# Context feed-forward: sums of w2 kept in four PSUM banks over all features, norm tiles lent to weights, decay polynomial issued earlier

## The chip, the cores and the metric

The kernel runs on one core of one Trainium2 chip. The metric is the device time of one execution, in microseconds. Before the change the median of three runs is 2177.3 us (2174.9 to 2180.68).

## The reference

One layer of a diffusion trunk works on 1024 latent tokens and 256 context tokens of width 1024. The stage in question is the first feed-forward, applied to the context:

```
h   = rms_norm(ctx, norm1_w) * (1 + scale) + shift
ctx = ctx + 0.5 * gate * ((silu(h @ w1) * (h @ w3)) @ w2)
```

w1 and w3 have 2816 columns, that is 22 features of 128; w2 has 2816 rows and 1024 columns. After it come the token mixing (retention heads with a decay per head, log_sigmoid of a small table; gated linear attention heads) and a second feed-forward for the latents. The updated context is needed for the mixing; its own second half is not computed.

## The kernel before

All matrices are in fp32. Every operand is split into a high part, which ScalarE writes (L60), and a low part, the rest, which VectorE or GpSimd subtracts (L61). One product is three matmuls (`mm3`, L65 to L67): high by high, high weight by low, low weight by high. Tokens stand on the free axis, so the context is a tile of 256 columns, and the residual stream x of the context is eight tiles of 128 x 256.

The latents' feed-forward runs first. Its w2 part (`back6`) computes six of seven products of a block scheme, in 11 pairs of features each. Behind it comes the context's feed-forward, the stage of the change, and behind that the seventh product (`prod(4)`), the context's keys and values, and the mixing.

In the context's stage a loop runs over f = 0, 2, ..., 20 (`classic`). For each of the features f and f+1 it loads the two halves of w1 (512 columns each) and runs one group of 24 matmuls into a bank of the pool psA (`H`), takes silu on ScalarE (`s1`), does the same with w3, multiplies on VectorE (`s3`, L587) and splits the result into g's high part (`ghi`, ScalarE) and low part (`glo`, VectorE). Between the two features it calls the w2 part of the pair before, `Y(f - 2)`. The last pair's is called in `prod(4)`'s feed.

`Y` (L591 to L614) loads w2 in four halves (two features by two halves of 512 columns). Each of eight units m takes a bank of the pool psB, runs six matmuls (two features, three each), and VectorE adds gate times the sum to x (L600). So a pair has 48 matmuls and eight additions, and the bank is free again when its addition is done.

Weights arrive by SyncE's queue into six `raw` buffers of 256 KB. The high and low parts of w1 and w3 go to the tiles `hh00` to `hh07` and `hl00` to `hl07` (`halves_slots`), which stand free in this stage; those of w2 go to six `whi` and six `wlo` buffers. GpSimd writes the low parts of w1 and w3, VectorE those of w2. Beside all this, VectorE and ScalarE compute the latents' norm (half 1) step by step, one step per pair (`pend`): the sum of squares is summed over partitions by TensorE (L187), `nr` is the power -1/2 of it on GpSimd (L1095), VectorE builds diagonal matrices from it (`ndiag`, L194), TensorE spreads them (L203), and then each of eight features is normed (L217, ScalarE, L223). These products use psB, as `psN` says, and the normed tiles `hh10` to `hl17` are all allocated ahead of the loop.

The order of each engine's instructions is set by a scheduler from the program order, priorities and the times at which it thinks buffers are free; each engine then executes its list in order and waits at the first instruction whose inputs are not there. SyncE's list is written in program order through `back6`.

`lg_setup` (L840 to L871) loads the decay table and computes log_sigmoid with a power on GpSimd and a polynomial in some 25 VectorE operations on tiles of 128 x 8; at L871 and L868 ScalarE takes exponentials of it. It is called by `mix_setup`, at the start of the mixing.

Of the kernel before, what the change touches and what calls it, by code (L numbers as in the profile page):

```python
# [11 lines left out]
F32 = mybir.dt.float32  # L12
F32R = mybir.dt.float32r
AF = mybir.ActivationFunctionType
ALU = mybir.AluOpType
PSUM = bass.MemoryType.PSUM

P = 128
D = 1024
KD = D // P  # L20
DFF = 2816
NF = DFF // P
NP = NF // 2
LAT = 1024
CTX = 256
# [6 lines left out]
class Trunk:  # L32
# [241 lines left out]
    def halves_slots(self, i):  # L274
        if i < 2:
            return None, None
        return tuple(self.hslot(f"0{2 * (i % 4) + j}") for j in range(2))

    def load_halves(self, src, dst=(None, None), eng=None):
        return [self.load_half(src[:, 512 * i:512 * i + 512], dst[i], eng) for i in range(2)]  # L280
# [212 lines left out]
    def back6(self, keep=True):  # L493
        A = self.bank4(self.psA)
        self.prod(1, A, True)
        c1 = self.keep4(A)
        B = self.bank4(self.psB)
        self.prod(2, B, True)
        self.add4(0, 0, self.plus4(c1, B))
        self.prod(6, A, False)  # L500
        u2 = self.keep4(A)
        B = self.bank4(self.psB)
        self.prod(5, B, True)
        c5 = self.keep4(B)
        self.prod(7, A, False)
        if keep:
            u3 = self.keep4(A)
            self.add4(1, 1, self.plus4(c5, u3))
        else:
            self.add4(1, 1, self.plus4(c5, A))  # L510
            self.add4(0, 1, A)
        self.prod(3, B, False)
        self.add4(1, 0, self.plus4(u2, B))
        return A
# [76 lines left out]
    def Y(self, f, order, after=None, qs=(0, 1)):  # L591
# [18 lines left out]
        if after:  # L610
            for tg, o, n in order:
                for m in range(KD):
                    unit(ws[m // 4], tg, o, n, m)
                after(tg, o, n)  # L614

    def H(self, w, tg):
        ps = self.psA()
        self.proj(w, tg, ps)
        return ps
# [217 lines left out]
            act(a, a, AF.Exp, scale=-1.0)  # L837
            act(a, a, AF.Ln, bias=1.0)

    def lg_setup(self):  # L840
        nc, I, cp = self.nc, self.I, self.cp2
        x = self.tile(cp, [P, 8], F32, "lgx")
        nc.sync.dma_start(x, I["decay"].broadcast_to([P, 8]))
        e = self.tile(cp, [P, 8], F32, "lge")
# [5 lines left out]
        t = self.tile(cp, [P, 8], F32, "lgt")  # L850
# [7 lines left out]
            nc.vector.tensor_scalar(out=e, in0=e, scalar1=1.0 / m, scalar2=None, op0=ALU.add)  # L858
        nc.vector.tensor_tensor(out=e, in0=e, in1=u, op=ALU.mult)
        nc.vector.tensor_scalar(out=x, in0=x, scalar1=0.0, scalar2=None, op0=ALU.min)  # L860
        nc.vector.scalar_tensor_tensor(out=x, in0=e, scalar=-2.0, in1=x, op0=ALU.mult, op1=ALU.add)
        self.lg = x
        self.kd = {}
        for i, (nm, s, pos) in enumerate((("f", 0, 2), ("f0", 0, 3), ("b", 4, 0), ("b1", 4, 1))):
            t = self.tile(cp, [P, 4], F32, "kd" + nm)
# [578 lines left out]
    def run(self):  # L1444
        nc, tc, I = self.nc, self.tc, self.I
        S = {}

        def opn(name, side="left"):
            S[name] = tc.tile_pool(name=name, bufs=1, reuse_waits="tile", side=side)
            return S[name].__enter__()  # L1450
# [22 lines left out]
        with tc.manual_schedule(engines={mybir.EngineType.PE, mybir.EngineType.DVE, mybir.EngineType.Activation}):  # L1473
            ws = self.first1((xp, xp, None), n1)
# [24 lines left out]
        hc = opn("hc", "right")  # L1499
        self.gp = hc  # L1500
        n2 = opn("n2", "right")
# [3 lines left out]
        plan = defaultdict(list)  # L1505
# [29 lines left out]
        norm2 = lambda tg, i: norm_step(tg, i, self.mcol(4, int(tg == 2)), self.mcol(3, int(tg == 2)))  # L1535
        for i, at in enumerate((24, 27, 30, *range(33, 33 + KD))):
            plan[at].append(lambda i=i: ctx1(i))

        CT = [(2, 0, 256)]
        p4 = 6 * NP  # L1540
        plan[p4 + 1] += [lambda: self.Y(NF - 2, CT), lambda: self.alloc_h((2,), hc), lambda: norm2(2, 0)]
        plan[p4 + 4].append(lambda: norm2(2, 1))
        plan[p4 + 6].append(lambda: norm2(2, 2))
        for k in range(KD):
# [22 lines left out]
        def spill(tg):  # L1567
            o = TGS[tg][0]
            for k in range(KD):
                nc.sync.dma_start(self.xd[k * P:(k + 1) * P, o:o + 512], self.x[tg][k])  # L1570

        self.alloc_h((1,), self.hp)
        norm2(1, 0)
        pend = [lambda i=i: norm2(1, i) for i in range(1, 3 + KD)] + [lambda: spill(1)]
        for f in range(0, NF, 2):
            self.classic(f, (2,), mid2=(lambda: self.Y(f - 2, CT)) if f else None, eng=[nc.gpsimd if e else None for e in CENG])
            pend.pop(0)()
        A = self.bank4(self.psA)
        self.prod(4, A, True)
        self.add4(0, 1, A)  # L1580
# [85 lines left out]
CENG = (1, 1, 1, 1)  # L1666
# [98 lines left out]
```

## Time and profile before

| what | value |
|---|---|
| median of three runs | 2177.3 us |
| profiled execution, its own time | 2180.54 us |
| its span | 2178.8 us |
| granted TensorE clock, mean | 0.99 |
| first L600 to last | 673.6 to 861.8 us |

The profile has one page and a trace behind it. The page gives busy time per engine, the span in 40 slices, the chain that ended last, and groups of equal instructions with their mean duration and the idle time ahead of them. Answers of the trace give single instructions: start, duration, engine, line, operation, output and inputs, and in brackets how long the engine sat idle before it and what ended that. A matmul's duration in the trace overlaps the next one's; their starts give the pace.

### The profile page before, as it was taken

How to read it: one execution, taken by the hardware profiler on the slowest of the kernel's cores; microseconds unless marked ns; L12 is line 12 of the kernel's file. 1: busy time of each engine (PE TensorE's matmuls, PEld its weight loads, DVE VectorE, ACT ScalarE, POOL GpSimd, SP SyncE). 2: the span in 40 equal slices, each digit the busy share in tenths (PEclk: the TensorE clock that was granted, in tenths of full speed). 3: DMA queues.
4: the chain of work that ended last, by engine and by line, in shares of the span. 5: the costliest groups of instructions: out<-in, count | busy, mean ns of one | idle time of the engine just before them, and what ended most of it. 6: DMA issues, size and time to landing. Idle time of an engine off the chain costs nothing. (4 is left out here: it accounts for less than half of the span.)

```text
span 2178.8 us, 32819 instructions
## 1 busy us (share of the span) xinstructions
PE 2121.3 (97%) x11558; PEld 1811.5 (83%) x11558; DVE 1525.0 (70%) x2735; ACT 980.7 (45%) x1811; POOL 280.4 (13%) x285
## 2 busy tenths in 40 slices
PE   8999999999999999999989999999999999999998
PEld 7888888888889999987778988788878888888888
DVE  7889999756766756834665546758777666675676
ACT  4433334345545444546454335425343433444553
POOL 0000000000026562611132113200000000010000
PEclk8999999999999999999999999999999999999999
DMA  9267768469966565553322312324134444467674
GB/s 331 83 231 239 267 221 268 167 221 325 306 210 193 156 183 171 180 152 100 92 65 63 98 57 88 122 83 162 63 120 161 146 160 159 150 217 251 207 241 147
DMA packets 202933, 373.39 MB, mean 171 GB/s; under 512 B 24016, under 2 KB 37264, under 8 KB 202768
## 3 DMA queue, kind: packets, MB, share of 16 engines
q1 hardware_dynamic: 202336, 371.16, 52.7%
q8 instruction: 90, 1.47, 0.3%
q14 instruction: 75, 0.61, 0.1%
q10 hardware_dynamic: 432, 0.13, 0.0%
HBM read 296.72 MB, written 66.09 MB: 167 GB/s over the span
## 5 line engine op out<-in xcount | busy, mean ns | idle before, releaser
L60 ACT ACTIVATE whi<-raw 128x512 fp32r<-128x512 f32 (+1 forms) x563 | 347.1, 622 | 621.1 <-PE psa L66 169.1
L61 DVE TENSOR_TENSOR wlo<-raw,whi 128x512 fp32r<-128x512 f32 (+1 forms) x533 | 368.1, 694 | 314.3 <-ACT whi L60 310.9
L65 PE MATMUL psa<-hh,whi 128*128 128x512 f32 (+1 forms) x1108 | 435.2, 393 | 0.1
L66 PE MATMUL psa<-hl,whi 128*128 128x512 f32 (+1 forms) x1108 | 434.6, 392 | 0.0
L67 PE MATMUL psa<-hh,wlo 128*128 128x512 f32 (+1 forms) x1108 | 434.3, 392 | 0.0
L65 PE MATMUL psb<-hh,whi 128*128 128x512 f32 (+1 forms) x680 | 260.0, 382 | 0.5 <-ACT whi L60 0.5
L67 PE MATMUL psb<-hh,wlo 128*128 128x512 f32 (+1 forms) x680 | 259.7, 382 | 0.6 <-DVE wlo L61 0.6
L66 PE MATMUL psb<-hl,whi 128*128 128x512 f32 (+1 forms) x680 | 259.7, 382 | 0.0
L65 PEld LDWEIGHTS psa<-hh,whi 128*128 128x128 f32 x1108 | 209.1, 189 | 42.1 <-ACT s L341 0.6
L67 PEld LDWEIGHTS psa<-hh,wlo 128*128 128x128 f32 x1108 | 209.0, 189 | 41.7
L66 PEld LDWEIGHTS psa<-hl,whi 128*128 128x128 f32 x1108 | 209.1, 189 | 41.3
L65 PEld LDWEIGHTS psb<-hh,whi 128*128 128x128 f32 x680 | 127.9, 188 | 25.9 <-ACT whi L60 1.0
L67 PEld LDWEIGHTS psb<-hh,wlo 128*128 128x128 f32 x680 | 127.8, 188 | 25.7 <-DVE wlo L61 1.0
L66 PEld LDWEIGHTS psb<-hl,whi 128*128 128x128 f32 x680 | 127.9, 188 | 24.8
L60 ACT ACTIVATE hh<-raw 128x512 fp32r<-128x512 f32 x180 | 110.4, 623 | 72.7 <-PE psa L66 44.3
L61 POOL TENSOR_TENSOR hl<-raw,hh 128x512 fp32r<-128x512 f32 x84 | 116.2, 1393 | 70.5 <-ACT hh L60 64.4
L1095 POOL TENSOR_TENSOR nr<-nr,mhalf 128x4 f32<-128x4 f32 (+1 forms) x11 | 10.6, 964 | 869.3 <-DVE nr L1094 869.3
L65 PE MATMUL psa<-hh,hh 128*128 128x256 f32 x376 | 107.8, 287 | 0.0
L67 PE MATMUL psa<-hh,hl 128*128 128x256 f32 x376 | 107.8, 287 | 0.0
L66 PE MATMUL psa<-hl,hh 128*128 128x256 f32 x376 | 107.8, 287 | 0.0
L66 PE MATMUL psa<-wlo,hh 128*128 128x256 f32 (+1 forms) x320 | 93.8, 293 | 1.6 <-DVE wlo L61 1.5
L65 PE MATMUL psa<-whi,hh 128*128 128x256 f32 (+1 forms) x320 | 93.5, 292 | 1.2 <-ACT s L1049 1.2
(402 smaller groups left out, 4251.7 us busy)
## 6 DMA issues: line engine op xcount, KB each, us to landing
raw<-in_w SPq DMA_DIRECT2D x374, 256.0 KB, 3.2
gd<-s SPq DMA_DIRECT2D x154, 256.0 KB, 2.8
ada<-in_adaT SPq DMA_DIRECT2D x76, 512.0 KB, 4.8
raw<-gd SPq DMA_DIRECT2D x91, 256.0 KB, 3.0
s<-in_w SPq DMA_DIRECT2D x66, 256.0 KB, 5.0
sd<-s SPq DMA_DIRECT2D x44, 256.0 KB, 2.9
raw<-sd SPq DMA_DIRECT2D x44, 256.0 KB, 3.1
hh<-in_w SPq DMA_DIRECT2D x44, 256.0 KB, 3.9
```

The costliest lines, as they stand in the source:

```text
L60: nc.scalar.activation(hi, src, AF.Copy)
L61: (eng or nc.vector).tensor_tensor(out=lo, in0=src, in1=hi.bitcast(F32), op=ALU.subtract)
L65: mm(ps, wa[0], xa[0], start=start, stop=False, skip_group_check=more)
L66: mm(ps, wa[0], xa[1], start=False, stop=False, skip_group_check=more)
L67: mm(ps, wa[1], xa[0], start=False, stop=stop, skip_group_check=more)
L1095: nc.gpsimd.tensor_tensor(out=r, in0=r, in1=self.mhalf[:, :n], op=ALU.pow)
```

## The change

Four things change. `Yc` takes the place of `Y` for the context: it takes four banks of psB at f = 0 and keeps all eight sums in them (two to a bank), through all 22 features; only in the last pair does VectorE add gate times the sum to x, eight times. The norm's products in the loop go to psA (`psN`). `norm1(k)` allocates the pair of tiles of a normed feature only when it is normed, and until then `halves_slots` lends the tiles `h1{p-2}` to one weight half of pair p, for p from 2 to 9. And the first part of `lg_setup` becomes `lg_start`, called after the loop's step f = 8, with its temporary tiles in the pool `n2`.

```diff
     def halves_slots(self, i):
         if i < 2:
             return None, None
-        return tuple(self.hslot(f"0{2 * (i % 4) + j}") for j in range(2))
+        p, last = i // 4, i % 4 == 3
+        return tuple(self.hslot(f"1{p - 2}" if last and j and 2 <= p < 10 else f"0{2 * (i % 4) + j}") for j in range(2))
...
+    def Yc(self, f):
+        if not f:
+            self.yb = self.bank4(self.psB)
+        ws = {q: [self.load_half(self.w2[f + i][:, 512 * q:512 * q + 512]) for i in range(2)] for q in range(2)}
+        for m in range(KD):
+            ps = self.yb[m // 2][:, m % 2 * CTX:(m % 2 + 1) * CTX]
+            for i in range(2):
+                self.mm3(ps, [t[:, m % 4 * P:(m % 4 + 1) * P] for t in ws[m // 4][i]], self.g[f + i, 2],
+                         not (f or i or m % 2), f == NF - 2 and i == 1, True)
+            if f == NF - 2:
+                x = self.x[2][m]
+                self.nc.vector.scalar_tensor_tensor(out=x, in0=ps, scalar=self.gates_m[1][:, m:m + 1], in1=x,
+                                                    op0=ALU.mult, op1=ALU.add)
...
-    def lg_setup(self):
-        nc, I, cp = self.nc, self.I, self.cp2
+    def lg_start(self, cp):
+        nc, I = self.nc, self.I
...
-        nc.vector.scalar_tensor_tensor(out=x, in0=e, scalar=-2.0, in1=x, op0=ALU.mult, op1=ALU.add)
-        self.lg = x
+        self.lg = self.tile(self.cp, [P, 32], F32, "lg")[:, :8]
+        nc.vector.scalar_tensor_tensor(out=self.lg, in0=e, scalar=-2.0, in1=x, op0=ALU.mult, op1=ALU.add)
+
+    def lg_setup(self):
+        nc, cp, x = self.nc, self.cp2, self.lg
...
-        CT = [(2, 0, 256)]
         p4 = 6 * NP
-        plan[p4 + 1] += [lambda: self.Y(NF - 2, CT), lambda: self.alloc_h((2,), hc), lambda: norm2(2, 0)]
+        plan[p4 + 1] += [lambda: self.Yc(NF - 2), lambda: self.alloc_h((2,), hc), lambda: norm2(2, 0)]
...
-        self.alloc_h((1,), self.hp)
+        self.h[1] = []
         norm2(1, 0)
-        pend = [lambda i=i: norm2(1, i) for i in range(1, 3 + KD)] + [lambda: spill(1)]
+
+        def norm1(k):
+            self.h[1].append(self.hslot(f"1{k}"))
+            norm2(1, 3 + k)
+
+        self.psN = self.psA
+        pend = [lambda i=i: norm2(1, i) for i in (1, 2)] + [lambda k=k: norm1(k) for k in range(KD)] + [lambda: spill(1)]
         for f in range(0, NF, 2):
-            self.classic(f, (2,), mid2=(lambda: self.Y(f - 2, CT)) if f else None, eng=[nc.gpsimd if e else None for e in CENG])
+            self.classic(f, (2,), mid2=(lambda: self.Yc(f - 2)) if f else None, eng=[nc.gpsimd if e else None for e in CENG])
             pend.pop(0)()
+            if f == 8:
+                self.lg_start(n2)
+        self.psN = self.psB
```

The scheduler moves instructions for it (in rows of the changed kernel the line numbers behind the new lines are up to 18 higher, so L1095 reads L1113 there). On TensorE, behind the group of f = 1's w3 (its last two rows come first in both lists; `psa_1373` and `psa_1357` are its bank), there stood before the first group of f = 2:

```order
L66 MATMUL psa_1373_6134<-hl27_823_4102,hh07_1369_6124 128x256
L67 MATMUL psa_1373_6134<-hh27_822_4101,hl07_1370_6125 128x256
L65 MATMUL psa_1384_6184<-hh20_808_4087,hh00_1378_6172 128x256
L66 MATMUL psa_1384_6184<-hl20_809_4088,hh00_1378_6172 128x256
L67 MATMUL psa_1384_6184<-hh20_808_4087,hl00_1379_6173 128x256
```

In the changed kernel Yc(0) stands there, with g of f = 0 (`ghi_1341`, `glo_1342`) and of f = 1 (`ghi_1358`, `glo_1359`; the list is cut at the thirteenth matmul, the first that reads `glo_1359`; the cut ones repeat the pattern for the second and third unit):

```order
L66 MATMUL psa_1357_6118<-hl27_823_4102,hh07_1353_6108 128x256
L67 MATMUL psa_1357_6118<-hh27_822_4101,hl07_1354_6109 128x256
L65 MATMUL psb_1379_6237<-ghi_1341_6063,whi_1384_6243 128x256
L66 MATMUL psb_1379_6237<-glo_1342_6064,whi_1384_6243 128x256
L67 MATMUL psb_1379_6237<-ghi_1341_6063,wlo_1385_6244 128x256
...
L65 MATMUL psb_1379_6237<-ghi_1358_6144,whi_1387_6249 128x256
L65 MATMUL psb_1380_6238<-ghi_1358_6144,whi_1387_6249 128x256
L65 MATMUL psb_1381_6239<-ghi_1358_6144,whi_1393_6261 128x256
L66 MATMUL psb_1379_6237<-glo_1359_6145,whi_1387_6249 128x256
```

So the sums of the first pair move ahead by four groups, 96 matmuls. Those of the second pair move ahead likewise, directly behind the group of f = 3's w3 (`psa_1409`) and three matmuls of the norm; before they stood behind groups of f = 4 and f = 5. The changed kernel's rows (`ghi_1377` is g of f = 2, `ghi_1410` and `glo_1411` that of f = 3):

```order
L67 MATMUL psa_1409_6364<-hh27_822_4101,hl07_1406_6355 128x256
L187 MATMUL psa_1360_6148<-ones_5_84,nacc1_1284_5800 128x1 x3
L65 MATMUL psb_1379_6237<-ghi_1377_6233,whi_1436_6492 128x256
...
L65 MATMUL psb_1381_6239<-ghi_1410_6390,whi_1445_6510 128x256
L66 MATMUL psb_1379_6237<-glo_1411_6391,whi_1439_6498 128x256
```

From Yc(4) on TensorE's order is as before. On GpSimd the norm's `nr` was, before, followed by the last weight split of f = 5 (`hl07_1486`) and preceded by that feature's first three:

```order
L61 TENSOR_TENSOR hl04_1476_6607<-raw_1479_6610,hh04_1475_6606 128x512
L61 TENSOR_TENSOR hl05_1478_6609<-raw_1480_6614,hh05_1477_6608 128x512
L61 TENSOR_TENSOR hl06_1484_6646<-raw_1487_6649,hh06_1483_6645 128x512
L1095 TENSOR_TENSOR nr_1377_6169<-nr_1377_6169,mhalf_6_86 128x4
L61 TENSOR_TENSOR hl07_1486_6648<-raw_1488_6653,hh07_1485_6647 128x512
```

Now all four precede it, and the one that is loaded last, into the lent tile `hl10`, comes first:

```order
L61 TENSOR_TENSOR hl10_1458_6604<-raw_1460_6609,hh10_1457_6603 128x512
L61 TENSOR_TENSOR hl04_1448_6563<-raw_1451_6566,hh04_1447_6562 128x512
L61 TENSOR_TENSOR hl05_1450_6565<-raw_1452_6570,hh05_1449_6564 128x512
L61 TENSOR_TENSOR hl06_1456_6602<-raw_1459_6605,hh06_1455_6601 128x512
L1113 TENSOR_TENSOR nr_1361_6153<-nr_1361_6153,mhalf_6_86 128x4
```

On ScalarE the four halves of w2 of the second pair (`whi_1436`, `whi_1439`, `whi_1442`, `whi_1445`) now stand together, with one weight half of f = 4 (`hh00`) between the last two and the other (`hh01`) behind them. SyncE's loads come in the order of before in this stage.

## The prediction

> **What bounds the kernel now.** I read the page's line of busy times first, to see whether one engine sets the end.
>
> ```profile
> PE 2121.3 (97%) x11558; PEld 1811.5 (83%) x11558; DVE 1525.0 (70%) x2735; ACT 980.7 (45%) x1811; POOL 280.4 (13%) x285
> ```
>
> TensorE is busy for 97% of the span of 2178.8 us. The change leaves the number of its weight products alone, so only two things can bring the end nearer: shorter gaps on TensorE, and less time at half clock. I therefore cut the context's feed-forward (until about 860 us) into stretches. The columns are start and end, length, then busy us and instructions of PE, PEld, DVE, ACT and POOL, then the granted clock, DMA share and GB/s.
>
> ```profile
> 660.00:680.00 20.00, 17.40 (x143) 16.99 (x142) 11.01 (x19) 10.62 (x22) 16.06 (x11) 1.00 0.65 199
> 680.00:700.00 20.00, 20.00 (x145) 20.00 (x144) 10.71 (x20) 8.62 (x16) 11.25 (x9) 0.83 0.57 177
> 700.00:720.00 20.00, 16.32 (x119) 16.12 (x118) 18.11 (x28) 9.17 (x17) 7.55 (x5) 0.85 0.41 119
> 720.00:740.00 20.00, 18.90 (x152) 18.49 (x152) 18.91 (x26) 10.62 (x20) 12.28 (x8) 0.98 0.51 154
> 740.00:760.00 20.00, 20.00 (x170) 20.00 (x168) 9.63 (x18) 9.24 (x18) 11.89 (x9) 1.00 0.61 189
> ```
>
> From 740 us on TensorE issues 170 matmuls in 20 us, 0.1176 us each. The four stretches ahead of that hold 143 + 145 + 119 + 152 = 559, where that pace would give 680. The 121 missing ones are **14.2 us**, all that this stage has to give. Then I asked the view by line who waits for the gated addition to x (L600): its row, and the engine that waited for it (us, times); and the timeline of TensorE for the four waits themselves (the bracket is idle time and releaser).
>
> ```profile
> L600 DVE SCALAR_TENSOR_TENSOR x<-psb,modc,x x88: 466/472/486, 673.6 to 861.8; 128x256 f32<-128x256 f32 x88
> ...
>   PE psb L65: 7.3, 4
> ```
>
> ```profile
> 674.15 0.39 PE L65 MATMUL psb<-ghi,whi 128*128 128x256 f32 x1 [0.72 <-DVE x L600]
> 679.17 0.39 PE L65 MATMUL psb<-ghi,whi 128*128 128x256 f32 x1 [1.88 <-DVE x L600]
> 715.15 0.58 PE L65 MATMUL psb<-ghi,whi 128*128 128x256 f32 x1 [3.67 <-DVE x L600]
> 736.15 0.39 PE L65 MATMUL psb<-ghi,whi 128*128 128x256 f32 x1 [0.99 <-DVE x L600]
> ```
>
> All 7.3 us fall into the first three pairs of features, where the latents' norm keeps VectorE full (18.1 and 18.9 of 20 us above) and L600 stands in its queue. The remaining 7 us are mostly half clock behind the waits, which finer stretches show:
>
> ```profile
> 675.00:680.00 5.00, 3.12 (x26) 2.91 (x25) 2.52 (x4) 3.14 (x6) 4.21 (x3) 0.99 0.58 182
> 680.00:685.00 5.00, 5.00 (x26) 5.00 (x25) 3.66 (x9) 1.39 (x3) 2.28 (x2) 0.50 0.55 178
> 715.00:720.00 5.00, 4.85 (x22) 4.85 (x23) 4.21 (x10) 0.72 (x1) 0.00 (x0) 0.50 0.13 46
> 720.00:725.00 5.00, 5.00 (x40) 5.00 (x40) 4.18 (x7) 2.57 (x5) 1.76 (x2) 0.92 0.32 105
> ```
>
> At full pace 5 us hold 42.5 matmuls. Behind the wait of 3.67 us the slow clock cost (42.5 - 22 + 42.5 - 40) x 0.1176 = 2.7 us, 2.6 without the wait's last 0.15.
>
> **What the change removes.** 80 of the 88 L600 go, and with them every wait for a bank that one of them holds: the sums lie in four banks until the last pair. That takes the waits and the slow clock behind them, **-14.2 us**. The 80 x 0.472 = 38 us of VectorE work saved count for no more than that, since TensorE waits for VectorE nowhere else in this stage. The last eight additions follow their sums one by one, as before: 0.
>
> **What it puts in: the first sums stand too early.** The instruction order puts Yc(0) directly behind f=1's second group, where four more groups (96 matmuls) used to be. In the trace that place is at 660.21; Yc(0)'s thirteenth matmul, twelve further on, would stand at 661.65, and it needs the low half of g of f=1.
>
> ```profile
> 660.21 0.28 PE L65 MATMUL psa<-hh,hh 128*128 128x256 f32 x1
> ...
> 661.65 0.28 PE L65 MATMUL psa<-hh,hh 128*128 128x256 f32 x1
> ```
>
> ```profile
> 662.42 0.42 ACT L60 ACTIVATE ghi<-s 128x256 fp32r<-128x256 f32 x1 [1.59 <-DVE s L587]
> 662.87 0.63 DVE L61 TENSOR_TENSOR glo<-s,ghi 128x256 fp32r<-128x256 f32 x1 [0.48 <-ACT ghi L60]
> 664.57 0.40 ACT L60 ACTIVATE ghi<-s 128x256 fp32r<-128x256 f32 x1
> 665.01 1.26 DVE L61 TENSOR_TENSOR glo<-s,ghi 128x256 fp32r<-128x256 f32 x1 [0.92 <-ACT ghi L60]
> ```
>
> VectorE's order up to these rows is the same in both kernels, so nothing brings them sooner: g's low half is there at 665.01 + 1.26 = 666.27, and TensorE is 4.6 us late. It waits in pieces (for 662.84, 663.50, 664.97 and 666.27), so half clock may add up to 2.6.
>
> **The second sums stand too early as well, and behind a longer chain.** Yc(2) follows f=3's second group directly. Its thirteenth matmul stands 158 behind Yc(0)'s start, so without any delay at 660.21 + 158 x 0.1176 = 678.8. It needs g of f=3, whose low half stands on VectorE behind the first `ndiag`, which waits for GpSimd's `nr`, and there four weight splits (f=5's) now stand ahead of `nr`, the first of them for the load that comes last. These are the rows for that chain; the two group rows have count, busy us and mean ns, and the DMA row size and median us to landing.
>
> ```profile
> 669.16 0.63 ACT L60 ACTIVATE whi<-raw 128x512 fp32r<-128x512 f32 x1 [3.66 <-DMA raw<-in_w]
> 669.88 0.69 DVE L61 TENSOR_TENSOR wlo<-raw,whi 128x512 fp32r<-128x512 f32 x1 [3.61 <-ACT whi L60]
> 671.29 0.97 DVE L61 TENSOR_TENSOR wlo<-raw,whi 128x512 fp32r<-128x512 f32 x1 [0.72 <-ACT whi L60]
> ```
>
> ```profile
> L61 POOL TENSOR_TENSOR hl<-raw,hh 128x512 fp32r<-128x512 f32 x84 | 116.2, 1393 | 70.5 <-ACT hh L60 64.4
> ...
> raw<-in_w SPq DMA_DIRECT2D x374, 256.0 KB, 3.2
> ```
>
> ```profile
> 682.02 0.16 DVE L1094 TENSOR_SCALAR nr<-psb 128x4 f32<-128x4 f32 x1 [0.44 <-PE psb L187]
> 682.26 1.01 POOL L1095 TENSOR_TENSOR nr<-nr,mhalf 128x4 f32<-128x4 f32 x1 [2.40 <-DVE nr L1094]
> 683.42 1.56 DVE L194 TENSOR_SCALAR ndiag<-ident,nr 128x128 f32<-128x128 f32 x2
> ```
>
> The four halves of w2 now stand together in ScalarE's order. The second one's low part ends at 671.29 + 0.97 = 672.26 and frees the buffer for the fourth; 3.2 for that load and 0.63 for its split give 676.1. Behind it ScalarE splits f=4's second half (0.63, 676.7), GpSimd takes 1.39 for its low part (678.1), and this frees the buffer of f=5's last load: 3.2 and 0.63 more, 681.9. Then four GpSimd splits (5.6, 687.5), `nr` (1.0), `ndiag` (0.8) and the low half of g (0.6): 689.9. So TensorE is **11.1 us** late there. This contains the 4.6 of Yc(0) and its half clock, which only shorten the second wait. Bounds: if the splits do not stand in the way, `nr` follows f=3's sum of squares at 660.21 + 4.6 + 145 x 0.1176 = 681.9, with 0.16 + 1.0 + 0.8 + 0.6 behind, hence 684.5 and 5.7 us; if each split takes the 2.26 of the slowest row (660.96, below), 3.5 more, 14.6. I take 11.1: it uses the mean row.
>
> ```profile
> 660.96 2.26 POOL L61 TENSOR_TENSOR hl<-raw,hh 128x512 fp32r<-128x512 f32 x1 [5.68 <-ACT hh L60]
> ```
>
> **Half clock behind Yc(2).** TensorE's wait there is 11.1 - 4.6 = 6.5 us, or 3.9 if Yc(0) already cost 2.6. The trace knows both outcomes: 3.67 us was followed by half clock (above), a lone 2.44 us at 1124.68 was not, as the stretch behind it shows.
>
> ```profile
> 1124.68 0.30 PE L1081 MATMUL psb<-ident,t 128*128 128x128 f32 x1 [2.44 <-DVE t L1327]
> ...
> 1126.00:1131.00 5.00, 5.00 (x34) 4.49 (x33) 4.59 (x9) 1.28 (x4) 0.00 (x0) 1.00 0.32 96
> ```
>
> Both waits are nearer to the first, so I take **2.6** (ends 0 and 2.6). The Trainium skill, "TensorE: Matmul & The Clock Gate" (section "Why this matters for your kernels"), warns of idle gaps over about 3 us alone. By that rule Yc(0)'s pieces, 2.4 us at most, cost no clock and Yc(2)'s 6.5 us do, so it speaks against this change at the same place. The trace agrees on the 3.67 and the 2.44; on the slow clock behind 0.72 and 1.88 us (680 us above) it goes beyond the rule.
>
> **The smaller edits.** One `ndiag` stands behind f=5's product on VectorE (0.41 + 0.78 at most, TensorE has a few matmuls in between): 0.5, ends 0 and 1.2. From Yc(4) on TensorE's order is the old one: 0. The decay's polynomial moves from the start of the mixing to the end of the first latents' stage.
>
> ```profile
> 937.41 0.40 PE L66 MATMUL psa<-wlo,hh 128*128 128x288 f32 x1 [1.18 <-DVE wlo L61]
> 941.03 0.21 ACT L871 ACTIVATE cdec<-lgx 128x8 f32<-128x8 f32 x1 [7.63 <-DVE lgx L861]
> 455.00:475.00 20.00, 20.00 (x89) 16.44 (x88) 12.84 (x20) 6.08 (x12) 0.00 (x0) 1.00 0.58 192
> ```
>
> There the weight split that TensorE awaits stands between its small operations: **-1.2** (0 if another wait takes the place). At its new place (about 458 to 472 us) VectorE has 7.2 of 20 us free and TensorE waits for nothing, so 0; if that cover were gone, up to 1.5, the wait for GpSimd's power in the chain. The small load passes SyncE's queue there once its buffer is free: in the same 0 to 1.5. The new slots for weight halves add no instruction; what they do to the order is in the chain above.
>
> **Sum:** -14.2 + 11.1 + 2.6 + 0.5 - 1.2 = **-1.2 us**. The profiled run was 2180.5 (span 2178.8), which gives 2179.3; against the median of 2177.3, **2176.1**.
>
> **Rivals.**
> - The short chain: f=5's loads come early enough, or its splits do not delay `nr`, and Yc(2) costs only the lower bound. -14.2 + 5.7 + 0.5 - 1.2 = -9.2, 2168.1; with half clock behind Yc(0), 2170.7. For it: GpSimd was busy for only 11.3 of 20 us at 680. Against: the rows of the chain.
> - The long chain without half clock behind it: -3.8, 2173.5.
> - Slower: the four w2 halves in a row make ScalarE wait in every pair. The third and fourth wait for a buffer that VectorE frees (0.69), a load (3.2) and a split (0.63): 4.5 us, in which the next pair's silu stands behind them, and the last group of that pair waits for the bank that this silu reads. One group (24 x 0.1176 = 2.8) lies between, so at most 1.7 us a pair, 15 in the nine pairs from Yc(4) on: 2191. It ends over 0.3% slower from 0.86 a pair. Against: ScalarE has over 10 of 20 us free at 740.
> - The change does not do what it says: L600 was only the last of several waits, and weights or g end as late. 2177. Against: the waits name L600 four times, and from 740 on, with the same loads, TensorE never waits.
>
> **How the numbers follow.** 0.3% (6.5 us) is about what a measurement of this kernel tells from no change. Forecast 0.37, short chain 0.30, long chain at full clock 0.15, slower 0.13, no effect 0.05. The short chain alone is faster by over 0.3%: 0.30; forecast, full clock and no effect lie within: 0.57; slower 0.13. The range runs from 2165 (the short chain with the decay's polynomial gaining more) to 2184: it takes in the chain's upper bound (+3.5, 2179.6) with 1.5 at the polynomial's new place and the clock's uncertain terms, and leaves out the 0.13 and a little of the short chain.
>
> **What would show it.** Right: no wait of TensorE for a gated addition before the last pair; idle time at about 660 to 666 and again at 683 to 690, the second released by g of f=3, with clock 0.50 behind it; 170 matmuls per 20 us from there on; no wait at the start of the mixing for the low half of a weight. Wrong: Yc(2) starting without a wait, or waits for silu in the later pairs.

## The result and the profile after

The changed kernel takes 2189.98 us (median of six runs, 2187.8 to 2195.8), the kernel before 2179.86 in the same comparison (six runs, 2174.9 to 2182.32). The ratio is 1.0053 with an interval of 1.0036 to 1.0069: **slower by 10 to 12 us** (10.1 by the medians, 11.6 by the ratio), where 2176.1 (2165 to 2184) was predicted. TensorE's busy time grew with the span (2188.4 us):

```profile
PE 2126.1 (97%) x11558; PEld 1808.4 (83%) x11558; DVE 1510.5 (69%) x2655; ACT 976.9 (45%) x1811; POOL 280.5 (13%) x285
```

The same stretches as in the prediction, and the four behind them, of the changed kernel (length; busy us and instructions of PE, PEld, DVE, ACT, POOL; granted clock; DMA share; GB/s):

```profile
660.00:680.00 20.00, 16.34 (x110) 15.54 (x110) 9.71 (x16) 9.29 (x18) 9.80 (x7) 0.83 0.62 193
680.00:700.00 20.00, 17.85 (x151) 17.65 (x150) 5.88 (x12) 8.24 (x16) 10.66 (x10) 1.00 0.52 161
...
740.00:760.00 20.00, 20.00 (x171) 20.00 (x170) 11.08 (x10) 8.50 (x18) 11.40 (x8) 1.00 0.53 170
760.00:780.00 20.00, 18.47 (x156) 18.26 (x155) 11.03 (x10) 9.53 (x20) 12.12 (x9) 1.00 0.51 159
780.00:800.00 20.00, 18.40 (x156) 18.19 (x154) 11.46 (x11) 9.73 (x21) 12.62 (x10) 1.00 0.52 159
800.00:820.00 20.00, 18.61 (x157) 18.41 (x156) 12.84 (x12) 9.26 (x19) 13.73 (x11) 1.00 0.57 175
820.00:840.00 20.00, 18.52 (x154) 18.11 (x152) 7.96 (x10) 8.71 (x17) 11.51 (x9) 1.00 0.60 187
```

Up to 680 us the cost stands where the prediction put it, and 740 to 760 is full. But the four stretches from 760 on lose some 1.5 us each, where the kernel before lost nothing (its row for the same 80 us):

```profile
760.00:840.00 80.00, 80.00 (x669) 80.00 (x668) 39.72 (x75) 39.13 (x75) 47.40 (x36) 1.00 0.61 182
```

The changed kernel's waits of TensorE in this stage, from its timeline:

```profile
664.52 0.58 PE L65 MATMUL psb<-ghi,whi 128*128 128x256 f32 x1 [3.56 <-ACT ghi L60]
...
689.75 0.39 PE L66 MATMUL psb<-glo,whi 128*128 128x256 f32 x1 [2.15 <-DVE glo L61]
...
766.24 0.39 PE L66 MATMUL psb<-glo,whi 128*128 128x256 f32 x1 [1.53 <-DVE glo L61]
...
785.19 0.38 PE L66 MATMUL psb<-glo,whi 128*128 128x256 f32 x1 [1.60 <-DVE glo L61]
...
803.92 0.39 PE L66 MATMUL psb<-glo,whi 128*128 128x256 f32 x1 [1.39 <-DVE glo L61]
...
821.54 0.39 PE L66 MATMUL psb<-glo,whi 128*128 128x256 f32 x1 [0.27 <-DVE glo L61]
...
841.07 0.38 PE L65 MATMUL psb<-ghi,whi 128*128 128x256 f32 x1 [2.28 <-ACT ghi L60]
```

No matmul waits for a gated addition any more. The first two waits are Yc(0)'s and Yc(2)'s; a norm product's wait of 0.45 us for `ndiag` at 707.14 is left out. The later ones lie 18 to 20 us apart, one in each pair of features, 7.1 us together; the sum had nothing for them.

To see where the 10 us arise, I set the two traces beside each other matmul by matmul (by line, operands and order) and subtracted the starts. The difference of the starts, changed minus before, grows in these stretches (times of the kernel before):

| stretch of the kernel before, us | growth, us | what lies there |
|---|---|---|
| 0 to 640 | +0.6 | latents' feed-forward |
| 640 to 748 | -4.5 | Yc(0), Yc(2), the L600 waits gone |
| 748 to 853 | **+9.1** | the waits in the pairs |
| 853 to 928 | +0.1 | seventh product |
| 928 to 958 | -1.3 | old place of the decay's polynomial |
| 958 to 1600 | +0.7 | mixing |
| 1600 to 1940 | **+4.5** | second feed-forward of the latents |
| 1940 to 2150 | +0.5 | end |

So there are two losses, and the second lies in a stage that the change does not touch. There TensorE waits for nothing in either kernel; its rows for 240 us of that stage, before and then changed:

```profile
1700.00:1940.00 240.00, 240.00 (x1061) 198.72 (x1060) 162.27 (x265) 97.99 (x170) 0.00 (x0) 1.00 0.47 155
```

```profile
1700.00:1940.00 240.00, 240.00 (x1047) 196.11 (x1046) 159.17 (x261) 94.41 (x164) 0.00 (x0) 1.00 0.45 148
```

Busy throughout at full clock, and still 14 matmuls fewer: 0.2267 us from start to start before, 0.2297 now. The groups say which. First the kernel before, then the changed one, in that window (count, busy us and mean ns):

```profile
L65 PE MATMUL psa<-hh,whi 128*128 128x512 f32 x104 | 40.5, 389 | 0.0
...
L67 PE MATMUL psa<-t3h,wlo 128*128 128x512 f32 x25 | 9.7, 389 | 0.0
```

```profile
L65 PE MATMUL psa<-hh,whi 128*128 128x512 f32 x104 | 40.5, 389 | 0.0
...
L67 PE MATMUL psa<-t3h,wlo 128*128 128x512 f32 x28 | 11.1, 395 | 0.0
```

Matmuls whose moving operand lies in `t1` to `t3` became slower, those with `hh` did not. Of the two groups of tiles, `hh` and the weights lie in pools that grow from the left, and `t1` to `t3` in one from the right. The change put the permanent tile `lg`, 128 bytes in each partition, ahead of the left ones: `hh00` moved from byte 3200 to 3328 and the first `whi` from 81024 to 81152, while `t1h0` stayed at 163712. The distance from weight to `t` went from a multiple of 256 bytes to 128 off one.

For the pairs I read ScalarE's timeline ahead of the wait at 766.24, then VectorE's, in the changed kernel:

```profile
759.76 1.67 ACT L60 ACTIVATE hh<-raw 128x512 fp32r<-128x512 f32 x3 [5.68 <-DMA raw<-in_w]
761.34 0.37 ACT L582 ACTIVATE s<-psa 128x256 f32<-128x256 f32 x1
```

```profile
761.74 0.42 DVE L588 TENSOR_TENSOR s<-psa,s 128x256 f32<-128x256 f32 x1 [5.76 <-ACT s L582]
762.93 1.85 DVE L223 SCALAR_TENSOR_TENSOR hl<-nt,modl,hh 128x512 fp32r<-128x512 f32 x1 [0.78 <-ACT hh L218]
764.71 1.48 DVE L61 TENSOR_TENSOR glo<-s,ghi 128x256 fp32r<-128x256 f32 x1
```

ScalarE sits idle for 5.68 us at a weight split that waits for its load. Two more splits and silu (L582) stand behind it, then VectorE's product, a norm step, and g's low half, which ends at 764.71 + 1.48 = 766.19; TensorE goes on at 766.24. The order shows which load it is. ScalarE's rows there in the changed kernel (`hh14` is the lent tile; `hh04`, `hh05` and `hh06` belong to the same feature):

```
L60 ACTIVATE hh14_1658_7597<-raw_1661_7603 128x512
L60 ACTIVATE hh04_1648_7556<-raw_1652_7560 128x512
L60 ACTIVATE hh05_1650_7558<-raw_1653_7564 128x512
L582 ACTIVATE s_1606_7353<-psa_1605_7328 128x256
L60 ACTIVATE hh06_1656_7595<-raw_1660_7599 128x512
```

The last number of a load gives its place in SyncE's order: the split that stands first needs the load that comes last (7603 behind 7560, 7564 and 7599). It can stand first because its tile is free early; a tile of the ring `hh00` to `hh07` comes free only when the pair before has used it.

The same order stands in all eight pairs with a lent tile, from f = 4 on. From the second of them on, ScalarE's wait at the lent half grows, and TensorE waits only from the 5.68 us above on (behind it they are 4.69, 4.55, 3.45 and 4.57). The three ahead of it:

```profile
702.52 1.68 ACT L60 ACTIVATE hh<-raw 128x512 fp32r<-128x512 f32 x3 [1.33 <-DMA raw<-in_w]
...
722.08 1.67 ACT L60 ACTIVATE hh<-raw 128x512 fp32r<-128x512 f32 x3 [2.42 <-DMA raw<-in_w]
...
739.79 1.67 ACT L60 ACTIVATE hh<-raw 128x512 fp32r<-128x512 f32 x3 [3.59 <-DMA raw<-in_w]
```

**Theory**: two separate causes. The lent tile's split stands ahead of its load's turn (about 9 us), and 128 bytes moved two operands of one matmul against each other (about 5 us). **Rivals**: the pair waits come from w2's four halves standing together (the prediction's slower case); the slower pace comes from something else that the change does, such as the early decay or the four banks; or Yc(0) and Yc(2) alone make the loss.

### The profile page after: what moved, and what is told of

Same layout as the page of the kernel before. It is cut to its first block, busy times and chain, and to the rows that moved or that the text cites. A ratio compares the mean times of both kernels' runs of the same rounds, so it can differ in the third digit from the quotient of the medians.

```text
span 2188.4 us, 32748 instructions
## 1 busy us (share of the span) xinstructions
PE 2126.1 (97%) x11558; PEld 1808.4 (83%) x11558; DVE 1510.5 (69%) x2655; ACT 976.9 (45%) x1811; POOL 280.5 (13%) x285
## 5 line engine op out<-in xcount | busy, mean ns | idle before, releaser
L61 DVE TENSOR_TENSOR wlo<-raw,whi 128x512 fp32r<-128x512 f32 (+1 forms) x533 | 375.9, 710 | 332.6 <-ACT whi L60 327.7
L65 PE MATMUL psa<-hh,whi 128*128 128x512 f32 (+1 forms) x1108 | 435.3, 393 | 0.0
L67 PE MATMUL psa<-hh,wlo 128*128 128x512 f32 (+1 forms) x1108 | 434.7, 392 | 0.0
L65 PE MATMUL psb<-hh,whi 128*128 128x512 f32 (+1 forms) x680 | 260.0, 382 | 0.5 <-ACT whi L60 0.5
L67 PE MATMUL psb<-hh,wlo 128*128 128x512 f32 (+1 forms) x680 | 259.9, 382 | 0.4 <-DVE wlo L61 0.4
L65 PEld LDWEIGHTS psa<-hh,whi 128*128 128x128 f32 x1108 | 209.2, 189 | 42.5 <-ACT s L342 0.4
L67 PEld LDWEIGHTS psa<-hh,wlo 128*128 128x128 f32 x1108 | 209.2, 189 | 41.9
L65 PEld LDWEIGHTS psb<-hh,whi 128*128 128x128 f32 x680 | 127.8, 188 | 26.3 <-ACT whi L60 1.0
L67 PEld LDWEIGHTS psb<-hh,wlo 128*128 128x128 f32 x680 | 127.7, 188 | 25.7 <-DVE wlo L61 0.8
L65 PE MATMUL psa<-hh,hh 128*128 128x256 f32 x376 | 106.2, 282 | 0.0
L67 PE MATMUL psa<-hh,hl 128*128 128x256 f32 x376 | 105.9, 282 | 0.0
L65 PE MATMUL psa<-whi,hh 128*128 128x256 f32 (+1 forms) x320 | 93.2, 291 | 3.3 <-ACT s L1067 3.0
L67 PE MATMUL psa<-whi,hl 128*128 128x256 f32 (+1 forms) x320 | 92.4, 289 | 0.0
```

The lines of the kernel that those rows point to most:

```text
L61: (eng or nc.vector).tensor_tensor(out=lo, in0=src, in1=hi.bitcast(F32), op=ALU.subtract)
L65: mm(ps, wa[0], xa[0], start=start, stop=False, skip_group_check=more)
L67: mm(ps, wa[1], xa[0], start=False, stop=stop, skip_group_check=more)
```

## The experiments

Twelve kernels ran, in three groups on one chip each, each group with its own runs of the kernel before. Before gave medians of 2177.18, 2179.32 and 2175.61 in the three, and single runs of one kernel lie up to 6.5 us from their median, so I compare ratios, above all between groups. The last three columns are growths from the aligned traces as in the table above, each against the one profiled execution of the kernel before.

| kernel | median, us | ratio to before (95%) | 640-748 | 748-853 | 1600-1940 |
|---|---|---|---|---|---|
| changed | 2189.98 | 1.0053 (1.0036 to 1.0069) | -4.5 | +9.1 | +4.5 |
| e1_addr | 2184.40 | 1.0036 (1.0022 to 1.0049) | -2.8 | +9.3 | 0.0 |
| e2_shift | 2186.49 | 1.0045 (1.0032 to 1.0058) | +1.5 | -1.1 | +4.5 |
| e3_nolend | 2176.47 | 0.9998 (0.9989 to 1.0007) | -6.7 | -1.2 | +4.5 |
| e4_lend | 2183.46 | 1.0026 (1.0015 to 1.0037) | -6.7 | +6.3 | 0.0 |
| e5_both | 2170.56 | 0.9967 (0.9956 to 0.9979) | -6.3 | 0.0 | 0.0 |
| e6_late | 2172.71 | 0.9973 (0.9964 to 0.9983) | -6.1 | 0.0 | 0.0 |
| e7_lendfirst | 2176.94 | 0.9992 (0.9983 to 1.0001) | -7.6 | 0.0 | +4.5 |
| e8_shift256 | 2182.68 (one run) | | -0.3 | 0.0 | 0.0 |
| e9_align | 2168.56 | 0.9966 (0.9953 to 0.9978) | -7.2 | 0.0 | 0.0 |
| e10_order | 2164.56 | 0.9949 (0.9935 to 0.9962) | -13.5 | 0.0 | 0.0 |
| e11_best | 2164.31 | 0.9948 (0.9935 to 0.9961) | -12.3 | 0.0 | 0.0 |
| e12_lg | 2182.28 | 1.0022 (1.0011 to 1.0033) | -2.2 | 0.0 | 0.0 |

The three growth columns are not equally sure. That one execution of the kernel before took 2180.54 us, some 3 us over its median. In 640 to 748 the kernels with TensorE's order of before and no lent tile (e2_shift, e8_shift256, e12_lg) scatter from -2.2 to +1.5, as the waits and the half clock behind them fall, so a difference of under some 4 us in that column shows nothing by itself. In the other two columns the kernels without a loss agree within about 0.1, but for the -1.1 and -1.2 that are explained below.

### The 128 bytes: e1_addr, e2_shift, e8_shift256

e1_addr is the changed kernel with `lg` in a pad at the right-hand edge, so that every other tile lies where it lay before; the order of all engines is that of the changed kernel.

```diff
-        self.lg = self.tile(self.cp, [P, 32], F32, "lg")[:, :8]
...
-        self.pad(edge, 24)
+        self.pad(edge, 16)
+        self.lg = self.tile(edge, [P, 8], F32, "lg")
```

> The changed kernel with the eight columns of `lg` kept in a corner of the right-hand pad instead of a tile of 128 bytes in the permanent pool. All weight, hidden and norm tiles of the feed-forwards stand at the addresses of before again; every engine's order is that of the changed kernel. Address theory (the 128-byte shift slows the 128x512 matmuls of the latents' feed-forwards): start to start 0.2267 us again in the second feed-forward (0.2297 after), about 5 us faster than the changed kernel, 2185 where that is 2190. Rival (the slower pace comes with the run, or from the loads): 2190, pace 0.2297.

e2_shift is the kernel before with an unused tile of 128 bytes in the same pool; e8_shift256 has one of 256 bytes (`[P, 64]`).

```diff
+        nc.gpsimd.memset(self.tile(cp, [P, 32], F32, "shift"), 0.0)
```

> The kernel before with an unused tile of 128 bytes per partition at the end of the permanent pool, so that the same tiles stand 128 bytes higher, as after; one memset on GpSimd at the start is added and every engine's order is else that of before. Address theory: 5 us slower than before, pace 0.2297 in the second feed-forward. Rival: as before, pace 0.2267.

> The kernel before with an unused tile of 256 bytes instead of the 128 of e2_shift; all orders as in e2_shift. If any shift of the weights against the unshifted tiles t1 to t3 slows those matmuls: 0.2297 us start to start at 1700 to 1940 us, 0.233 with t1 to t3. If only some distances do (weights and t lie 256 bytes apart modulo 512 before, 128 in the changed kernel, 0 here): 0.2267.

The same 240 us in e1_addr, e2_shift and e8_shift256:

```profile
1700.00:1940.00 240.00, 240.00 (x1060) 198.82 (x1059) 161.08 (x264) 97.64 (x170) 0.00 (x0) 1.00 0.47 152
```

```profile
1700.00:1940.00 240.00, 240.00 (x1047) 196.12 (x1046) 158.65 (x260) 94.89 (x165) 0.00 (x0) 1.00 0.44 147
```

```profile
1700.00:1940.00 240.00, 240.00 (x1060) 198.80 (x1059) 161.15 (x264) 97.64 (x170) 0.00 (x0) 1.00 0.46 152
```

1060, 1047, 1060, against 1061 before and 1047 after. An unused tile of 128 bytes alone brings the slow pace into the kernel before, one of 256 bytes does not, and the change at its old addresses has the old pace. So the pace of this stage hangs on the distance of the operands, and not on the change's work. By the ratios the shift is worth 0.0017 in the changed kernel (1.0053 against 1.0036, 3.7 us) and 0.0031 without the lending (e3_nolend against e5_both below, 6.7 us); the traces have 4.5. The 9.3 us (2186.49 - 2177.18) that e2_shift lost are more than its 4.5 here and 1.3 ahead of 640 us; its trace has 3.1 more in the mixing. But e8_shift256, at the old pace, has 1.9 there, and e5_both 2.6, so that part is no effect of the pace. In e2_shift and e5_both 1.6 of it is half clock behind one wait, the 2.44 us at 1124.68 of the kernel before, which came in seven of the fourteen traces and not in the others; the rest stays open.

Nor does a shift by 128 bytes always cost. In the pairs the 128x256 matmuls of e2_shift and e3_nolend start every 118.7 ns, where the kernel before has 120.0; that is their -1.1 and -1.2 in 748 to 853. e7_lendfirst, with the same shift, has 118.7 only until about 700 us and then 120.0, so distance alone doesn't settle the pace there.

### The lent tile: e3_nolend, e7_lendfirst, e4_lend

e3_nolend is the changed kernel without the lending. e7_lendfirst lends the same tiles to the half that is loaded first of the four instead of last.

```diff
-        p, last = i // 4, i % 4 == 3
-        return tuple(self.hslot(f"1{p - 2}" if last and j and 2 <= p < 10 else f"0{2 * (i % 4) + j}") for j in range(2))
+        return tuple(self.hslot(f"0{2 * (i % 4) + j}") for j in range(2))
```

> The changed kernel without the lending: weight halves go to the tiles 00 to 07 only, as before; Yc, the norm on psA and the early decay stay. TensorE's, GpSimd's and SyncE's orders are those of the changed kernel, ScalarE's and VectorE's differ in some twenty rows. Lending theory (ScalarE's splits for a lent tile stand ahead of silu and wait there for their load): the five waits of 1.4 to 2.3 us for g in the pairs after 760 us and the half clock at 840 go, 7 to 9 us faster than the changed kernel. Rival (Yc itself, or its w2 halves in a row, make g late in each pair): the waits stay, within 1 us of the changed kernel. The first two waits (665 and 689 us) stay in both.

```diff
-        p, last = i // 4, i % 4 == 3
-        return tuple(self.hslot(f"1{p - 2}" if last and j and 2 <= p < 10 else f"0{2 * (i % 4) + j}") for j in range(2))
+        p, lend = i // 4, i % 4 == 2
+        return tuple(self.hslot(f"1{p - 2}" if lend and not j and 2 <= p < 10 else f"0{2 * (i % 4) + j}") for j in range(2))
```

> The changed kernel with the lent tile given to the first-loaded half of f + 1 in each of the pairs 2 to 9 (w1's, instead of w3's second, which is loaded last of the four). Addresses as after. Order theory (the harm comes from the last-loaded half standing first in ScalarE's order, silu behind it): the waits for g after 760 us go although a tile is lent, and the time is within 2 us of e3_nolend, 2176.5. Rival (the lending itself harms, by the norm's steps or by buffers held): the waits stay, 2184 to 2190.

e4_lend is the kernel before with the lending and the late allocation of the norm's tiles alone.

> The kernel before with the lending alone: weight halves of pairs 2 to 9 in tiles 10 to 17 until these are normed; Y and its additions as before. Only ScalarE's and VectorE's orders differ from before, by some twenty rows. Lending theory: waits of TensorE for g appear in the pairs after 760 us, 5 to 9 us slower than before. Rival (the waits need Yc): no wait for g, 0 to 1 us from before.

The stretch of the pairs in e3_nolend, e7_lendfirst and e4_lend:

```profile
760.00:840.00 80.00, 80.00 (x677) 80.00 (x676) 30.26 (x44) 39.22 (x75) 42.63 (x32) 1.00 0.61 186
```

```profile
760.00:840.00 80.00, 80.00 (x669) 80.00 (x669) 33.96 (x47) 40.40 (x78) 43.19 (x32) 1.00 0.58 177
```

```profile
760.00:840.00 80.00, 77.63 (x630) 75.83 (x629) 49.18 (x81) 37.88 (x74) 45.33 (x32) 1.00 0.55 172
```

Without the lending, or with it for the first-loaded half, TensorE never idles here; with it alone, in the kernel before, it does. By the ratios e3_nolend is 0.0055 (12 us) faster than the changed kernel, more than the 7 to 9 us expected, and e7_lendfirst lies within 0.0006 of e3_nolend: the lending costs by its place in the order, not by its presence. In the traces 10.3 us of the difference to e3_nolend lie in the pairs and 2.2 at 640 to 748, where the wait at 689.75 is. This also rules out the first rival: in e3_nolend ScalarE still waits for w2's loads (27.7 us in 15 waits over 650 to 845 us), and TensorE does not wait for ScalarE in the pairs. e4_lend lost 6.3 us by time, and 6.3 in the pairs by its trace. The expectation had waits for g there; in fact there is one, of 1.12 us at 835.83, and the others are for gated additions, which are still there in this kernel (1.05 us at 747.58, 0.51 at 765.99, the rest about 0.1). So it shows that the lending costs without Yc, but in part through other waits; that e4_lend's profiled execution was still no longer (span 2177.9) comes from 640 to 748 us, where that one execution lost less to half clock (granted 0.98 over 660 to 760, before 0.93), and one profile can't tell whether the next would.

The lending also made the wait at 689.75: in e3_nolend TensorE's waits for g add up to this in the whole stage, 0.20 of it at Yc(2), where the changed kernel has 2.15 at Yc(2) alone:

```profile
PE psb L65 <- ACT ghi L60: 3.6, 1, 3.6
PE psb L66 <- DVE glo L61: 0.5, 2, 0.2
```

It made it on VectorE. The rows for `nr`, `ndiag` and g's low half, in the changed kernel and then in e3_nolend:

```profile
688.02 1.01 POOL L1113 TENSOR_TENSOR nr<-nr,mhalf 128x4 f32<-128x4 f32 x1
...
689.07 0.29 DVE L194 TENSOR_SCALAR ndiag<-ident,nr 128x128 f32<-128x128 f32 x1 [2.81 <-POOL nr L1113]
689.27 0.42 DVE L61 TENSOR_TENSOR glo<-s,ghi 128x256 fp32r<-128x256 f32 x1
```

```profile
687.78 1.22 DVE L61 TENSOR_TENSOR glo<-s,ghi 128x256 fp32r<-128x256 f32 x1 [0.25 <-ACT ghi L60]
...
688.68 1.19 POOL L1112 TENSOR_TENSOR nr<-nr,mhalf 128x4 f32<-128x4 f32 x1
...
689.90 0.48 DVE L194 TENSOR_SCALAR ndiag<-ident,nr 128x128 f32<-128x128 f32 x2 [0.90 <-POOL nr L1112]
```

GpSimd's `nr` comes no sooner without the lending, since the four splits stand ahead of it there too. But in the changed kernel the first `ndiag` stands ahead of g's low half, which so waits for `nr`; in e3_nolend it stands behind.

### Both undone, and the early sums: e5_both, e6_late, e10_order

e5_both joins the edits of e1_addr and e3_nolend.

> e1_addr and e3_nolend together: the changed kernel without the lending and with the tiles at the addresses of before. If the two causes add: 5 to 6 us below e3_nolend (2176.5), so 2171, and the decay's early start still gains 1.3 at 940 us. If the slower pace of e3_nolend's second feed-forward hid something else: 2174 to 2177.

It is **faster than the kernel before** (0.9967), so four banks over all features do pay, with the early decay that it still has (its stretch at 928 to 958 gains 1.6 us). What is left in its stage is Yc(0)'s wait (3.4 us) and half clock behind it. e6_late is e5_both with Yc(0) and Yc(2) at a low priority, so that the scheduler puts their matmuls where their inputs are ready.

```diff
+    def Yl(self, f):
+        with self.low(100 if f < 4 else None):
+            self.Yc(f)
```

> e5_both with Yc(0) and Yc(2) at a lower priority in the scheduler, so that Yc(0) stands behind the groups of f = 3, where Y(0) stood before, and Yc(2) behind f = 5 and 6. Early-sums theory (their place costs 4.6 us of waiting and 2.3 at half clock at 665 us): no wait at 661 to 669 us, no half clock there, 6 us below e5_both. Rival (the sums only wait elsewhere, for w2's buffers or for nr): 0 to 2 us below, with new waits of TensorE before 740 us.

Its waits of TensorE from 650 to 865 us (us in total, times, longest):

```profile
PE psa L187 <- DVE nacc L178: 2.9, 1, 2.9
PE psa L203 <- DVE ndiag L194: 2.5, 2, 2.3
PE psa L65 <- ACT s L581: 0.2, 1, 0.2
```

The waits moved on to the norm's products (L187, L203), which now came too early in their turn: 5.6 us in place of 3.6, and no gain. e10_order therefore moves all of it: TensorE keeps program order in the loop, the norm's steps come one pair later, and the store of x (`spill`) comes behind the loop.

```diff
-        pend = [lambda i=i: norm2(1, i) for i in (1, 2)] + [lambda k=k: norm1(k) for k in range(KD)] + [lambda: spill(1)]
-        for f in range(0, NF, 2):
-            self.classic(f, (2,), mid2=(lambda: self.Yc(f - 2)) if f else None, eng=[nc.gpsimd if e else None for e in CENG])
-            pend.pop(0)()
-            if f == 8:
-                self.lg_start(n2)
+        pend = [lambda: None] + [lambda i=i: norm2(1, i) for i in (1, 2)] + [lambda k=k: norm1(k) for k in range(KD)]
+        with self.pe_order():
+            for f in range(0, NF, 2):
+                self.classic(f, (2,), mid2=(lambda: self.Yc(f - 2)) if f else None, eng=[nc.gpsimd if e else None for e in CENG])
+                pend.pop(0)()
+                if f == 8:
+                    self.lg_start(n2)
+            spill(1)
```

> e5_both with TensorE's order in the context's loop written out in program order, and the norm's steps one pair later: Yc(0) stands behind f = 2's two groups, the sum of squares behind f = 3's. Early-place theory, with what e6_late taught (the norm's product must move too): no wait at 661 to 669 us and no half clock, 5 us below e5_both's 2170.6. Rival (each move uncovers the next wait): a wait of about the same size elsewhere before 740 us, 0 to 2 us.

All of TensorE's waits in its stage (650 to 865 us), and the first 100 us of it:

```profile
PE psa L203 <- DVE ndiag L194: 0.3, 1, 0.3
```

```profile
660.00:760.00 100.00, 99.67 (x832) 99.47 (x831) 57.92 (x75) 55.15 (x107) 69.43 (x49) 1.00 0.62 192
```

TensorE is full at clock 1.00, and the stage gains 13.5 us against the kernel before. By time it is 11.1 us faster than before (2164.56 against 2175.61).

### Another distance, the best version, and the decay alone: e9_align, e11_best, e12_lg

In the first feed-forward the tiles of x lie 224 bytes off a multiple of 256 from the weights (96 off in the changed kernel). e9_align is e5_both with an empty tile of 224 bytes ahead of them.

```diff
+        self.tile(self.dp, [P, 56], F32, "gap")
```

> e5_both with 224 bytes more in the right-hand pool of the first feed-forward, so that there the sixteen x tiles stand a multiple of 256 bytes from the weight tiles (96 modulo 256 instead of 128 before, against weights at 128). All orders unchanged. Distance theory (a matmul is slower where its two operands' distance is no multiple of 256 bytes): matmuls with x as operand at 200 to 400 us go from about 0.234 to 0.227 us, some 2 us below e5_both. Rival (x is slow there for another reason, as its loads): no difference.

(The expectation has the two residues the wrong way round: x stood at 96 modulo 256 and now stands at 128, as the weights do.) The x matmuls in 120 to 440 us, before and then in e9_align:

```profile
L65 PE MATMUL psa<-x,whi 128*128 128x512 f32 x50 | 20.2, 404 | 0.0
...
L67 PE MATMUL psa<-x,wlo 128*128 128x512 f32 x50 | 19.8, 396 | 0.0
```

```profile
L65 PE MATMUL psa<-x,whi 128*128 128x512 f32 x54 | 21.5, 398 | 0.0
...
L67 PE MATMUL psa<-x,wlo 128*128 128x512 f32 x53 | 20.6, 389 | 0.0
```

They became faster and its trace is 3.3 us ahead of before by 640 us, where e5_both was 0.5 behind. But the ratio (0.9966) is e5_both's (0.9967): by time the gain isn't shown. e11_best joins e9_align and e10_order:

> e9_align and e10_order together. If both theories hold: 7 us below e5_both, 2163 to 2164. If only one: 2166 to 2169.

At 0.9948 (0.9935 to 0.9961) it beats both kernels, and can't be told from e10_order. e12_lg is the kernel before with the early decay alone (`lg_start` behind f = 8, `lg` in the right-hand pad).

> The kernel before with the early decay alone, its result in a corner of the right-hand pad, so that nothing is shifted. Expected from the prediction's term: the wait of 1.18 us for the low half of a weight at 937 us goes, 1.2 to 1.6 us below before. Rival (the chain delays VectorE where it now stands): as before or slower, with a wait of TensorE at 455 to 480 us.

It was slower, 1.0022. The rival had that, but for another reason: at the polynomial's new place its trace gained no wait. The old wait at 937 us is gone, but a few us earlier there is one that the kernel before does not have (the changed kernel has up to 1.7 us there, e5_both 1.32):

```profile
934.18 0.61 PE L65 MATMUL psa<-whi,hh 128*128 128x288 f32 x1 [2.86 <-ACT s L1051]
```

Half clock followed (0.50 over 934 to 939 us). The trace is 2.6 us further behind at 958 us than at 928, and ends 1.0 behind; the time is 6.7 behind by the medians (2182.28 against 2175.61), 4.8 by the ratio. One profile doesn't explain that, and it stays open.

## Why the prediction was wrong, step by step

- **The removed waits, -14.2: right.** No wait for a gated addition is left. e10_order, which has nothing in their place, gains 13.5 in that stretch. The prediction's 0.1176 us a matmul came from counts that take in the matmuls over both ends of a stretch; from start to start it is 0.120. By that the 14.2 would be 14.5, and the 2.7 for half clock 3.1, since a full 5 us show 44 matmuls and not 42.5.
- **Yc(0), 4.6 late and half clock up to 2.6: right in size, not in form.** Between the last matmul ahead of Yc(0) (660.67) and the first norm sum behind f = 3's groups (685.34) lie 145 others; at 0.120 us a start that is 17.5 us, and it took 24.7, so the loss was some 7.2. The prediction had the wait in pieces. But g of f = 0 came at 664.47 and not at 662.84, so TensorE stood still for 3.56 us in one go, and half clock followed at once; the slow matmuls then hid the wait for g of f = 1 (ready at 667.85 and not 666.27, thirteenth matmul at 667.91). The changed kernel:

```profile
665.00:670.00 5.00, 4.91 (x22) 4.51 (x21) 1.74 (x3) 1.60 (x4) 3.92 (x3) 0.50 0.64 189
670.00:675.00 5.00, 5.00 (x39) 5.00 (x39) 1.39 (x2) 1.44 (x3) 0.00 (x0) 0.89 0.43 118
...
690.00:695.00 5.00, 5.00 (x44) 5.00 (x44) 1.39 (x2) 1.86 (x3) 0.00 (x0) 1.00 0.42 123
```

- **Yc(2), ready at 689.9: right**, chain and time: four splits, `nr`, the first `ndiag`, and g's low half, which released TensorE at 689.75. What put g behind `ndiag` was the lending, by VectorE's order, as e3_nolend shows; the lent tile's load at the head of GpSimd's splits is not the reason, since `nr` is as late without it.
- **Half clock behind Yc(2), +2.6: did not come.** Yc(0)'s had already come and left a wait of 2.15 us only: 44 matmuls in the 5 us behind it. It was a near thing, for in e1_addr the wait there was 2.86 us and half clock followed (0.70 over 690 to 695). So the stretch holds -14.2, some 7.2 for Yc(0), 2.15 for Yc(2) and the 0.45 at `ndiag` (forecast 0.5), together -4.4; the trace has -4.5, where the prediction's terms added up to 0.
- **The decay, -1.2:** the stretch around its old place gained 1.3 us, as forecast. But e2_shift and e8_shift256, which leave the decay alone, show 0.8 and 0.3 there, so 0.5 to 1.0 is its own; and alone (e12_lg) it did not pay.
- **"From Yc(4) on TensorE's order is the old one: 0": failed, +9.1.** TensorE's order was the old one; ScalarE's was not. The step held the lent slots to "add no instruction" and looked for their effect in one place, the chain at Yc(2), while ScalarE's list has the last-loaded half first, with silu behind, in all eight pairs with a lent tile. The rival of 2191 had the mechanism (ScalarE waits for a load with silu behind) and, with 1.7 us a pair, about the price, but the wrong load: w2's halves make ScalarE wait in e3_nolend too, and TensorE nowhere in the pairs. That its 2191 is so near the measured 2189.98 is luck, since 4.5 us of the loss lie in another stage.
- **A term that was missing: +4.5.** All durations were taken from the trace of before, as if a matmul's were its own. The diff shows a new permanent tile of 128 bytes, and the prediction gave it no price.

## What to carry to other kernels

A tile that is free early lets a scheduler move its instruction to the head of an in-order list; give it to the operand that is loaded first, and compare each engine's order with the order of the loads, in every pair, not only where TensorE's own list changes. Ahead of pricing a change by old durations, see whether it moves tiles: a small permanent one shifts everything that is allocated behind it, and here 128 bytes changed the pace of matmuls in two stages, slower in one and faster in the other, where 256 bytes changed it in neither. Sums that are moved earlier wait for their inputs until all that stands in order around them moves with them (e6_late against e10_order).

## What the runs showed of the hardware

- The pace of a 128x512 matmul depended on the distance of weights and moving operand in the partition: in the second feed-forward 389 ns in the groups at multiples of 256 bytes (before, e1_addr, e8_shift256), 394 to 395 at 128 off (changed). In the first one, x at 224 off (before) and at 96 off (changed) had 404 for its L65 group and 396 for its L67 group; when the gap made the distance a multiple of 256 they had 398 and 389. The 128x256 matmuls of the context went the other way, 120.0 ns from start to start at a multiple of 256 and 118.7 at 128 off, with e7_lendfirst as an exception. Only these distances were tried, and why it is so, no run tells.
- Half clock: 3.56 us of idle time was followed by it (22 matmuls in 5 us, clock 0.50), 2.15 us at 689.75 was not. The Trainium skill, "TensorE: Matmul & The Clock Gate" (section "Why this matters for your kernels"), warns of gaps over about 3 us, and these two agree. So do all twelve waits of over 3 us in the context's stage of the fourteen traces (3.01 to 3.73): half clock followed each. Below that it went either way. The 2.28 us at 841.07 went beyond the rule; the stretch behind it in the changed kernel:

```profile
843.00:848.00 5.00, 5.00 (x36) 5.00 (x35) 2.75 (x6) 2.10 (x4) 0.00 (x0) 0.79 0.40 116
```

  Nor does the length of a wait under 3 us decide. The prediction took the 2.44 us at 1124.68 as a case without half clock; the same wait in the changed kernel, 2.48 us at 1127.37, was followed by it:

```profile
1128.00:1133.00 5.00, 5.00 (x23) 4.22 (x22) 4.07 (x9) 1.66 (x5) 0.00 (x0) 0.66 0.38 108
```

  In seven of the fourteen traces it was, in seven not, so one trace of a wait between 2 and 3 us can't tell what the next execution does.
